# MLP up and FFN gate/value products as seven block products of summed weights

## The chip, the cores and the metric

One core of a Trainium2 chip runs the program. The time is the device time of one execution in microseconds (us), the median of the executions measured.

## The reference

Two transformer blocks over 512 tokens of width 1024, in float32. What matters here are three products with two factors each: the MLP of the first block and the gated FFN of the second block, which comes twice.

```python
m = rms_norm(h, mlp_norm[i])
h = h + jnp.square(jax.nn.relu(m @ w_mlp_up[i])) @ w_mlp_down[i]      # 1024 -> 4096 -> 1024
...
def conv_ffn(h, w_gate, w_val, conv_w, conv_b, w_out):               # 1024 -> 2816 -> 1024
    a = h @ w_gate
    ap = jnp.pad(a, ((0, 0), (CONV_W - 1, 0), (0, 0)))
    a = ap[:, 0:S] * conv_w[0] + ap[:, 1:S + 1] * conv_w[1] + ap[:, 2:S + 2] * conv_w[2] + conv_b
    return (jax.nn.silu(a) * (h @ w_val)) @ w_out
```

Everything else (gated linear attention, latent attention, pooling, chunked attention) stays as it is.

## The kernel before

The stages follow one another: mix, mlp, ple, pool, ffn0, att, ffn1. The residual x lies as 8 tiles of 128 features x 512 tokens (`x_...`). Products are made at float32 accuracy: each factor is split into a high part (rounded to fp32r) and a low part (what is left), and `mm3` (L328) sums high·high, high·low and low·high in one PSUM bank:

```python
mm(out, a[0], b[0], start=start, stop=False, skip_group_check=True)
mm(out, a[0], b[1], start=False, stop=False, skip_group_check=True)
mm(out, a[1], b[0], start=False, stop=stop, skip_group_check=True)
```

Weights come in units of 1024 columns (512 KB). `load_units` (L247) loads one into a tile `ws` from SyncE's queue, at most NL = 3 ahead. `split_unit` (L257) makes the parts in two halves: ACT copies `wh`, VectorE (DVE) subtracts `wl` (or GpSimd, POOL, where the planner finds that sooner: `sub`, L304). NW = 4 pairs exist, and after the first stage a unit is split at most two units before its use (`LAZY`).

At a stage's start `prep` (L376) takes each new x tile as it becomes final: `xsh` by ACT, `xsl` by DVE, squares, and POOL sums them (`sq`); from the sum comes the row R = 1/rms, which is multiplied in when a product is taken from PSUM. An up tile (128 outputs x 512 tokens, tile `pup`; `pf` for gate and value) is one unit: 8 k-blocks x 3 = 24 matmuls of 512 columns. `products` (L1162) runs a stage's first two tiles together, one k-block at a time; `mlp` (L1184) and `ffn` (L1348) take the others in groups of about eight tiles. From a gate tile come `fa`, the convolution `fb` (one ACT and two DVE instructions), its silu; from a value tile `fv`, the product with `fb`, and the split `yh`, `yl`. `down` (L1142) multiplies a group's results into 8 outputs (tile `pdn`), one unit each, after the next group's up tiles (`weave`, L1136), and `add_to` (L421) adds each output to its x tile. The last group's outputs start the next stage.

What each engine does, and in which order, is written by tasks (`spawn`, L185; `drive`, L197): Python generators with priorities that advance by the planner's own costs (`Pace`, L60). The engines then run these lists in order, so an instruction that waits holds all behind it on its engine. Nearly every instruction is recorded at the planner's line, L133 before and L144 after the change.

Of the kernel before, what the change touches and what calls it, by code (L numbers as in the profile page):

```python
# [16 lines left out]
P = 128  # L17
T = 512
# [27 lines left out]
G1 = groups(FF1 // P, 8)  # L46
G2 = groups(FF2 // P, 8)
# [12 lines left out]
class Pace:  # L60
# [21 lines left out]
    def note(self, engine, op, args, kw):  # L82
# [11 lines left out]
        elif engine == "vector":  # L94
            fast = op in ("tensor_copy", "tensor_scalar") and all(x.space == "SB" or "SB" in str(x.space) for x in aps)
            cost = 0.068 + (m if op == "tensor_reduce" else n) / (1920 if fast else 960)
            if any(n > 1 and x.free_size() == 1 for x in ins):
                cost += 0.063
        elif engine == "scalar":
            cost = 0.09 + n / 1190 + (0.093 if len(outs) > 1 or hasattr(kw.get("scale"), "tensor") else 0)  # L100
        elif engine == "gpsimd":
            cost = 0.23 + 0.165 * n if kw.get("op") == OP.pow else 0.1 + n / (350 if ins else 1400)
        else:
            cost = outs[0].shape[0] * n * 4 / 360e3
# [7 lines left out]
        if engine == "tensor":  # L112
            self.mine.add(outs[0].tensor.name)
        self.free[engine] = start + cost
# [5 lines left out]
        for x in outs:  # L120
            self.ready[x.tensor.name] = start + cost + (2.0 if engine == "sync" else 0.08)
# [22 lines left out]
class Norm:  # L144


    def __init__(self, gain):
        self.gain, self.xs, self.acc, self.count = gain, [None] * KD, None, 0
        self.ms = self.r = self.R = None

# [9 lines left out]

class Block:
    NS, N3, NSM = 64, 8, 48
    NW, NL = 4, 3
# [6 lines left out]
    HELP, TURN = 0.0, 1.0  # L170

    def __init__(self, ctx, tc, a):
# [9 lines left out]
        self.done, self.lazy = set(), self.LAZY[0]  # L182
# [42 lines left out]
    def slot3(self, name, dt=F32, shape=(P, 768)):  # L225
# [20 lines left out]

    def load_units(self, most=None):  # L247
        while self.n_load < min(self.n_split + self.NL, len(self.units)) and (most is None or self.n_load < most):
            src, cols = self.units[self.n_load]
            t = self.sp.tile([P, 1024], F32, tag="ws", bufs=self.NL, name="ws")  # L250
            if self.n_load >= self.NL:
                self.pace.ready[t.tensor.name] = self.split_at[self.n_load - self.NL]
            self.nc.sync.dma_start(t[:, :cols], src)
            self.loaded[self.n_load] = t
            self.n_load += 1

    def split_unit(self):  # L257
# [3 lines left out]
        cols = self.units[n][1]  # L261
        t = self.loaded.pop(n)
# [9 lines left out]
        self.split_at.append(self.pace.ready[l.tensor.name])  # L272
# [3 lines left out]
    def splitter(self):  # L276
        while self.n_split < len(self.units):
            yield lambda: self.n_split - self.n_free < self.NW and self.n_split - self.n_use < self.lazy
            self.load_units()
            yield [self.loaded[self.n_split]] + ([self.freed_by[self.n_split - self.NW]] if self.n_split >= self.NW else [])  # L280
            self.split_unit()

    def unit(self, *shape):
# [4 lines left out]
        cols = self.units[n][1]  # L288
# [15 lines left out]
    def sub(self, out, a, b):  # L304

        e = self.first((out, a, b), vector=(0.07, 1 / 960, 0), gpsimd=(0.1, 1 / 430, self.HELP))
        getattr(self.nc, e).tensor_sub(out, a, b)

    def mul(self, out, a, b):

        e = self.first((out, a, b), vector=(0.07, 1 / 960, 0), gpsimd=(0.1, 1 / 430, self.HELP))
# [64 lines left out]
    def prep(self, norm, d, x, row=True):  # L376
        yield [x]
        norm.xs[d] = self.hilo("xs", x, scale=self.col(norm.gain, d))
        self.square(norm, x, row)

# [747 lines left out]

    def units_mlp(self):
        a = self.a  # L1130
        ups = [[(a["w_up"][i], 1024) for i in g] for g in G1]
        downs = [[(a[f"w_down{gi}"][m], len(g) * 128) for m in range(KD)] for gi, g in enumerate(G1)]
        return self.weave(ups, downs)

    @staticmethod
    def weave(ups, downs):  # L1136
        out = list(ups[0])
        for i in range(1, len(ups)):
            out += ups[i] + downs[i - 1]
        return out + downs[-1]  # L1140

    def down(self, acts, after):  # L1142
        for m in range(KD):
            yield from self.unit(len(acts), 128)
            unit = self.got
            yield self.room()
            ps = self.bank("pdn")
            yield from self.fm(ps, unit, acts)
            self.used(ps)
            self.spawn(self.add_to(m, ps, after), 0)  # L1150
# [10 lines left out]

    def products(self, norm, name, finish, first):  # L1162

        if first:
            units = []
            for f in finish[:2]:
                yield from self.unit(8, 128)
                units.append(self.got)
            yield self.room()
            ps = [self.bank(name) for u in units]  # L1170
            for k in range(KD):
                yield norm.has(k)
                x = norm.xs[k]
                for i, u in enumerate(units):
                    yield [*u, *x]
                    self.mm3(ps[i], (u[0][:, k], u[1][:, k]), x, k == 0, k == KD - 1)
            for p, f in zip(ps, finish):
                self.used(p)
                self.spawn(f(p), 0)
            finish = finish[2:]  # L1180
        for f in finish:
            yield from self.product(norm, name, f)

    def mlp(self, norm, after):  # L1184
        v, s = self.nc.vector, self.nc.scalar

        def finish(acts, i, ps):
            yield norm.has_row
            yield [ps, norm.R]
            t = self.slot3("ht")[:, :T]  # L1190
            v.scalar_tensor_tensor(t, ps, 0.0, norm.R, op0=OP.max, op1=OP.mult)
            self.free()
            yield [t]
            s.activation(t, t, AF.Square)
            acts[i] = self.hilo("h", t)

        pend = None
        for gi, g in enumerate(G1):
            acts = [None] * len(g)
            yield from self.products(norm, "pup", [lambda ps, acts=acts, i=i: finish(acts, i, ps) for i in range(len(g))],  # L1200
                                     gi == 0)
            if gi == len(G1) - 1:
                norm.xs = None
                self.spawn(self.load_p(), 5)
            if pend is not None:
                yield from self.down(pend, lambda m: None)
            pend = acts
        yield from self.down(pend, after)
# [133 lines left out]
    def units_ffn(self, L):  # L1342
        a = self.a
        ups = [sum(([(a[f"w_fg{L}"][i], 1024), (a[f"w_fv{L}"][i], 1024)] for i in g), []) for g in G2]
        downs = [[(a[f"w_fo{L}_{gi}"][m], len(g) * 128) for m in range(KD)] for gi, g in enumerate(G2)]
        return self.weave(ups, downs)

    def ffn(self, L, norm, after):  # L1348
        v, s = self.nc.vector, self.nc.scalar
        cw = [lambda i, t=t: self.col(f"cw{L}", t * 22 + i) for t in range(3)]  # L1350

        def gate(i, ps, got):
            yield norm.has_row
            yield [ps, norm.R]
            a, b = self.slot3("fa")[:, :T], self.slot3("fb")[:, :T]
            v.tensor_mul(a, ps, norm.R)
            self.free()
            yield [a]
            s.activation(b, a, AF.Identity, scale=cw[2](i), bias=self.col(f"cb{L}", i))
            yield [b]  # L1360
            v.scalar_tensor_tensor(b[:, 1:], a[:, :T - 1], cw[1](i), b[:, 1:], op0=OP.mult, op1=OP.add)
            v.scalar_tensor_tensor(b[:, 2:], a[:, :T - 2], cw[0](i), b[:, 2:], op0=OP.mult, op1=OP.add)
            yield [b]
            s.activation(b, b, AF.Silu)
# [344 lines left out]
```

## Time and profile before

| | before |
|---|---|
| runs, median of three (lowest, highest) | 1692.51 us (1686.52, 1693.08) |
| the profiled execution: its own time | 1687.25 us |
| its span | 1685.5 us |
| TensorE (PE) busy, matmuls | 1654.5 us (98%), 8696 |
| DVE busy, instructions | 1006.8 us (60%), 1889 |
| ACT busy, instructions | 728.5 us (43%), 1422 |
| POOL busy, instructions | 192.0 us (11%), 206 |
| loads on SyncE's queue (q1) | 152.30 MB, 28.5% of 16 DMA engines |
| mean granted clock of PE | 0.998 |

Spans are of one execution; the time is that execution's own and lies 1.75 us above its span. A PE that is busy nearly all the time says that the other engines' busy shares are free until they make PE wait.

### The profile page before, as it was taken

The page shows a single profiled execution, that of the slowest core. Times are in us where ns is not written, and L with a number is a line of the kernel's source. Part 1 is how long each engine was busy: PE and PEld are TensorE (multiplying, and loading weights), DVE is VectorE, ACT ScalarE, POOL GpSimd, SP SyncE. Part 2 cuts the span into 40 slices and gives each one's busy share as a digit, 9 for nine tenths or more (in the row PEclk, how much of TensorE's full clock was granted, in tenths as well). Part 3 has the DMA queues.
Part 4 walks back from the last instruction along what each step waited for, and adds up shares of the span by engine and source line. Part 5 has one row for each costly group of instructions (what it writes and reads, how often), then busy time and mean ns, then how long its engine had stood idle before and what let it go on. Part 6 is the DMA issues. An engine that isn't in the chain of part 4 may idle for free. (4 is left out here: it accounts for less than half of the span.)

```text
span 1685.5 us, 22515 instructions
## 1 busy us (share of the span) xinstructions
PE 1654.5 (98%) x8696; PEld 1391.6 (83%) x8696; DVE 1006.8 (60%) x1889; ACT 728.5 (43%) x1422; POOL 192.0 (11%) x206
## 2 busy tenths in 40 slices
PE   8999999999999999999999999999999999999999
PEld 6878777888888888888888888999998788888887
DVE  6986777443434456776654645376678776644642
ACT  6746445432324245643332333375656543322321
POOL 3441302000000012200000001122221200000000
PEclk9999999999999999999999999999999999999999
DMA  6102032332333223233332332322131232333232
GB/s 214 63 26 63 16 123 75 100 101 87 102 99 113 88 88 104 75 100 98 91 111 88 96 98 94 113 76 89 64 99 53 81 101 94 100 106 95 93 98 72
DMA packets 47501, 153.73 MB, mean 91 GB/s; under 512 B 5521, under 2 KB 7458, under 8 KB 47394
## 3 DMA queue, kind: packets, MB, share of 16 engines
q1 hardware_dynamic: 47394, 152.30, 28.5%
q8 instruction: 68, 1.11, 0.3%
q14 instruction: 39, 0.32, 0.1%
HBM read 150.18 MB, written 2.10 MB: 90 GB/s over the span
## 5 line engine op out<-in xcount | busy, mean ns | idle before, releaser
L133 ACT ACTIVATE wh<-ws 128x512 fp32r<-128x512 f32 (+1 forms) x536 | 302.6, 613 | 254.7 <-PE pdn L133 214.0
L133 DVE TENSOR_TENSOR wl<-ws,wh 128x512 fp32r<-128x512 f32 (+1 forms) x508 | 341.6, 713 | 113.0 <-ACT wh L133 112.7
L133 PE MATMUL pf<-xsl,wh 128*128 128x512 f32 x704 | 275.1, 391 | 2.0 <-DVE xsl L133 2.0
L133 PE MATMUL pf<-xsh,wh 128*128 128x512 f32 x704 | 275.9, 392 | 0.0
L133 PE MATMUL pf<-xsh,wl 128*128 128x512 f32 x704 | 274.6, 390 | 0.0
L133 DVE TENSOR_TENSOR x<-x,pdn 128x512 f32<-128x512 f32 (+1 forms) x81 | 55.1, 681 | 219.1 <-PE pdn L133 219.1
L133 PEld LDWEIGHTS pf<-xsl,wh 128*128 128x128 f32 x704 | 132.6, 188 | 32.0 <-DVE xsl L133 4.3
L133 PEld LDWEIGHTS pf<-xsh,wh 128*128 128x128 f32 x704 | 132.5, 188 | 28.5 <-issue 0.5
L133 PEld LDWEIGHTS pf<-xsh,wl 128*128 128x128 f32 x704 | 132.5, 188 | 27.3
L133 PE MATMUL pdn<-yh,wh 128*128 128x512 f32 x352 | 136.9, 389 | 0.0
L133 PE MATMUL pdn<-yl,wh 128*128 128x512 f32 x352 | 136.9, 389 | 0.0
L133 PE MATMUL pdn<-yh,wl 128*128 128x512 f32 x352 | 136.9, 389 | 0.0
L133 POOL TENSOR_TENSOR sq<-sq 128x512 f32<-128x512 f32 x37 | 52.8, 1427 | 731.0 <-ACT sq L133 730.0
L133 PE MATMUL paq<-wh,xsh 128*128 128x256 f32 x384 | 111.3, 290 | 1.9 <-DVE akk L133 1.2
L133 PE MATMUL paq<-wl,xsh 128*128 128x256 f32 x384 | 108.5, 283 | 0.0
L133 PE MATMUL paq<-wh,xsl 128*128 128x256 f32 x384 | 108.5, 283 | 0.0
L133 PE MATMUL pup<-xsl,wh 128*128 128x512 f32 x256 | 99.7, 389 | 0.4 <-DVE xsl L133 0.4
L133 PE MATMUL pup<-xsh,wh 128*128 128x512 f32 x256 | 100.1, 391 | 0.0
L133 PE MATMUL pup<-xsh,wl 128*128 128x512 f32 x256 | 99.6, 389 | 0.0
L133 PE MATMUL pdn<-hh,wh 128*128 128x512 f32 x256 | 99.6, 389 | 0.0
L133 PE MATMUL pdn<-hl,wh 128*128 128x512 f32 x256 | 99.6, 389 | 0.0
L133 PE MATMUL pdn<-hh,wl 128*128 128x512 f32 x256 | 99.6, 389 | 0.0
(293 smaller groups left out, 3103.5 us busy)
## 6 DMA issues: line engine op xcount, KB each, us to landing
ws<-in_w_fg SPq DMA_DIRECT2D x44, 512.0 KB, 3.6
ws<-in_w_fv SPq DMA_DIRECT2D x44, 512.0 KB, 3.6
ws<-in_w_up SPq DMA_DIRECT2D x32, 512.0 KB, 3.5
ws<-in_w_down SPq DMA_DIRECT2D x32, 512.0 KB, 3.5
ws<-in_w_fo SPq DMA_DIRECT2D x32, 448.0 KB, 3.3
ws<-in_w_fo SPq DMA_DIRECT2D x16, 512.0 KB, 3.5
ws<-in_w_out SPq DMA_DIRECT2D x8, 512.0 KB, 3.6
ws<-in_w_gate SPq DMA_DIRECT2D x8, 512.0 KB, 3.6
```

The lines of the kernel that those rows point to most:

```text
L133: return call(*args, **kw)
```

## The change

Four up tiles make a quad. With x as 2 x 2 blocks (k-blocks 0-3 and 4-7, tokens 0-255 and 256-511) and the weights of a quad as 2 x 2 blocks (k-blocks 0-3 and 4-7, output tiles 0-1 and 2-3), the 2 x 2 block product is made from seven products of sums instead of eight. Each is a phase: one unit of weights (a block, or a sum of blocks) times 4 k-blocks of 256 columns: 4 x 2 x 3 = 24 matmuls of 256 columns. Where a phase stands on an older result, that one is first taken from PSUM by an ACT copy (`c1`, `u2`, `u4`), and DVE combines.

- The first four tiles of each stage are done plainly and together (`first_tiles`): 96 matmuls of 512 columns, one k-block of four banks at a time. The other 28 tiles of mlp are 7 quads, the other 40 of each FFN 10 quads: 27 quads in all.
- Sums of weight blocks are made by DMA: a tile is loaded plainly, and other blocks are added into it by accumulating DMAs, which POOL issues. Per quad: 5 plain loads and 4 accumulating ones (one into `low`; into `sum` one at its load, one after the split of phase 2, one after that of phase 3) in place of 4 plain loads.
- `prep_blocks` builds the sums and differences of x blocks at a stage's start and splits them.
- The results of four tiles (mlp: one quad; FFN: two quads, since half of a quad's tiles are gates) are one down group. A down unit gives two outputs of four terms, and is woven in after phases 4, 3, 2 and 6 of the quads of the next group, as far as there are units: after phases 3 and 4 in most FFN quads, after all four in the mlp and in the ninth quad of an FFN, after phase 4 alone in quads 0, 1 and 9. x tiles are added to 64 times in mlp (32 before) and 56 times in each FFN (24 before).
- NL becomes 7, the 512-wide slots 55 (64 before), and after the first stage POOL no longer takes subtractions or products (`HELP`).

```diff
-    NS, N3, NSM = 64, 8, 48
-    NW, NL = 4, 3
+    NS, N3, NSM = 55, 8, 48
+    NW, NL = 4, 7
...
-    HELP, TURN = 0.0, 1.0
+    HELP, TURN = (0.0, 1e3), 1.0
...
+QG1 = [1] * (FF1 // P // 4)
+QG2 = [1] + [2] * (FF2 // P // 4 - 1) + [1] * 2
+
+PHASES = (("b11", 0, True, "a11"), ("b21", 1, True, "a12"), ("n3", 2, True, "sum"), ("n2", 0, False, "sum"),
+          ("n1", 0, False, "low"), ("b22", 0, False, "sum"), ("t4", 2, False, "a22"))
+
+LOADS = (("sum", 0, -2, (2,)), ("a11", 0, 0, ()), ("a12", 1, 1, ()), ("low", 2, 2, (3,)), ("a22", 3, 5, ()))
+
+ADDED = {2: 3, 3: 1}
...
+    def load_units(self, most=None):
...
+                n.tile[name] = t
+                for block in more:
+                    self.nc.gpsimd.dma_start(t, n.src[block], accum_op=OP.add)
...
+    def split_unit(self):
...
+            if ph in ADDED:
+                nc.gpsimd.dma_start(t, quad.src[ADDED[ph]], accum_op=OP.add)
...
+    def blocks_high(self, norm, k, x, col, h, l):
...
+        n, c = self.slot("xn"), self.slot("xc")
+        self.scaled(n, x, col)
+        nc.vector.scalar_tensor_tensor(c[:, L], low[:, R], -1.0, n[:, R], op0=OP.mult, op1=OP.subtract)
+        nc.vector.tensor_add(c[:, R], c[:, L], low[:, L])
+        nc.vector.tensor_add(n[:, L], n[:, L], c[:, L])
...
+    def quads(self, norm, order, sizes, last, after, take, finish):
...
+            if first:
+                yield self.room()
+                ps[acc] = self.bank("pq%d" % acc)
+            else:
+                name = (None, None, None, "c1", "u2", "u4", "c22")[i]
+                yield lambda: name in quad
+                yield [quad[name]]
+            b = norm.blocks[block]
+            for k in range(4):
+                yield lambda: b[k] is not None
+                for w in range(2):
+                    yield [*unit, *b[k]]
+                    self.mm3(ps[acc][:, w * 256:(w + 1) * 256], (unit[0][:, 4 * w + k], unit[1][:, 4 * w + k]), b[k],
+                             first and k == 0 and w == 0, k == 3)
...
+    def quad_step(self, i, ps, quad):
...
+        if i in (0, 3, 4):
+            name = {0: "c1", 3: "u2", 4: "u4"}[i]
+            t = self.slot(name)
+            s.activation(t, ps[0], AF.Copy)
+            quad[name] = t
+        if i == 1:
...
+            v.tensor_add(t, ps[1], t)
...
+        elif i == 4:
+            yield [t, ps[2]]
+            v.tensor_sub(t, ps[2], t)
+            quad["c22"] = t
...
+        elif i == 6:
+            t = quad["u2"]
+            yield [t, ps[2]]
+            v.tensor_sub(t, ps[2], t)
```

**In the middle of ffn1, on DVE.** Names: `qr` is a pair of result tiles (`qr_16430` the two value tiles of a quad, `fb_...` their gates), `pq0` to `pq2` the three banks, `ws_16121` the tile of `sum`. Before, one gate and one value tile:

```order
L133 TENSOR_TENSOR fa_12976<-pf_12924,R_12456 128x512
L133 SCALAR_TENSOR_TENSOR fb_12977<-fa_12976,cols_63,fb_12977 128x511
L133 SCALAR_TENSOR_TENSOR fb_12977<-fa_12976,cols_63,fb_12977 128x510
L133 TENSOR_TENSOR wl_13006<-ws_12891,wh_13005 128x512 x2
L133 TENSOR_TENSOR fv_13016<-pf_12964,R_12456 128x512
L133 TENSOR_TENSOR fv_13016<-fv_13016,fb_12977 128x512
L133 TENSOR_TENSOR yl_13023<-fv_13016,yh_13022 128x512
```

Now, from the last half of a quad's value tiles to their low parts, in the next quad:

```order
L144 TENSOR_TENSOR qr_16430<-u2_16351,R_14583 128x2x256
L144 TENSOR_TENSOR wl_16579<-ws_16121,wh_16578 128x512 x2
L144 TENSOR_TENSOR qr_16430<-qr_16430,fb_16501 128x512
L144 TENSOR_TENSOR wl_16597<-ws_16342,wh_16596 128x512 x2
L144 TENSOR_TENSOR c1_16563<-pq1_16558,c1_16563 128x512
L144 TENSOR_TENSOR yl_16624<-qr_16430,yh_16623 128x512
L144 TENSOR_TENSOR qr_16430<-qr_16430,fb_16536 128x512
L144 TENSOR_TENSOR wl_16635<-ws_16306,wh_16634 128x512 x2
L144 TENSOR_TENSOR qr_16643<-c1_16563,R_14583 128x2x256
L144 TENSOR_TENSOR wl_16671<-ws_16416,wh_16670 128x512 x2
L144 TENSOR_TENSOR yl_16679<-qr_16430,yh_16678 128x512
```

The split `wl_16579` of the sum for phase 3, made from what an accumulating DMA has added to, now stands ahead of the 13 instructions that end with the last low part of the values.

**At the start of ffn1.** DVE before, from the row's mean square to the first gates:

```order
L133 TENSOR_SCALAR ms_12415<-pst_12410 128x4
L133 TENSOR_TENSOR wl_12430<-ws_12270,wh_12429 128x512 x2
L133 TENSOR_SCALAR dg_12437<-ident_65,r_12417 128x128 x4
L133 TENSOR_TENSOR fa_12464<-pf_12331,R_12456 128x512
L133 TENSOR_TENSOR fv_12467<-pf_12332,R_12456 128x512
```

DVE now, the same stretch (`xc`, `xt`: sums of x blocks):

```order
L144 TENSOR_SCALAR ms_14506<-pst_14501 128x4
L144 TENSOR_TENSOR xcl_14511<-xc_14428,xch_14510 128x512
L144 TENSOR_TENSOR xt_14514<-xn_14427,xt_14514 128x256
L144 TENSOR_TENSOR wl_14527<-ws_14097,wh_14526 128x512 x2
L144 TENSOR_SCALAR dg_14549<-ident_65,r_14508 128x128 x4
L144 TENSOR_TENSOR wl_14567<-ws_13781,wh_14566 128x512 x2
L144 TENSOR_TENSOR xsl_14247<-xn_14252,xsh_14246 128x256
L144 TENSOR_TENSOR xsl_14259<-xn_14266,xsh_14258 128x256
L144 TENSOR_TENSOR xsl_14293<-xn_14300,xsh_14292 128x256
L144 TENSOR_TENSOR xsl_14319<-xn_14326,xsh_14318 128x256
L144 TENSOR_TENSOR qr_14560<-pf_14332,R_14583 128x512
```

Work on x blocks stands between the row and the first results, and more of it ahead of this stretch. From the first `xsl` to the low part that the first down output waits for, DVE's list holds 88 instructions in ffn1 and 86 in ffn0. POOL's list there is now

```order
L144 TENSOR_TENSOR sq_14250<-sq_14250,sq_14371 128x512
L144 DMA ws_14414<-in_w_f1 128x1024
L144 TENSOR_TENSOR r_14508<-ms_14506,mhalf_72 128x4
L144 DMA ws_13781<-in_w_f1 128x1024 x2
L144 DMA ws_14655<-in_w_f1 128x1024
```

where an accumulating DMA stands before the power that gives R, and four to a quad follow.

**At the end of ffn1, on DVE.** Before, splits and additions took turns, and all activations were long made:

```order
L133 TENSOR_TENSOR wl_14777<-ws_14688,wh_14776 128x448 x2
L133 TENSOR_TENSOR x_2706<-x_2706,pdn_14745 128x512
L133 TENSOR_TENSOR wl_14807<-ws_14720,wh_14806 128x448 x2
L133 TENSOR_TENSOR x_2769<-x_2769,pdn_14775 128x512
L133 TENSOR_TENSOR x_2797<-x_2797,pdn_14805 128x512
```

Now, from the last quad's seventh phase on:

```order
L144 TENSOR_TENSOR u2_17747<-pq2_17677,u2_17747 128x512
L144 SCALAR_TENSOR_TENSOR fb_17892<-qr_17706,cols_63,fb_17892 128x511
L144 SCALAR_TENSOR_TENSOR fb_17892<-qr_17706,cols_63,fb_17892 128x510
L144 TENSOR_TENSOR x_2789<-x_2789,pdn_17881 128x512
L144 TENSOR_TENSOR qr_17794<-u2_17747,R_14583 128x2x256
L144 TENSOR_TENSOR x_2815<-x_2815,pdn_17898 128x512
L144 TENSOR_TENSOR x_2878<-x_2878,pdn_17908 128x512
L144 TENSOR_TENSOR qr_17794<-qr_17794,fb_17862 128x512
L144 TENSOR_TENSOR x_2986<-x_2986,pdn_17917 128x512
L144 TENSOR_TENSOR yl_17930<-qr_17794,yh_17929 128x512
L144 TENSOR_TENSOR qr_17794<-qr_17794,fb_17892 128x512
L144 TENSOR_TENSOR yl_17938<-qr_17794,yh_17937 128x512
```

Between the last phase and the last down units only one down unit (four outputs) is left for PE.

## Rows read from the trace of the kernel before

**Rows 1.** The page, part 1: busy time, share of the span, instructions of each engine

```profile
PE 1654.5 (98%) x8696; PEld 1391.6 (83%) x8696; DVE 1006.8 (60%) x1889; ACT 728.5 (43%) x1422; POOL 192.0 (11%) x206
```

**Rows 2.** Waits of PE: for what, us in total, times, longest

```profile
PE pl L133 <- ACT wh L133: 8.4, 1, 8.4
PE pf L133 <- DVE xsl L133: 2.0, 3, 0.8
```

**Rows 3.** Stretches, PE alone: length, busy us (matmuls), granted clock, DMA share, GB/s

```profile
264.00:282.00 18.00, 15.87 (x71) 1.00 0.19 58
694.00:706.00 12.00, 10.77 (x48) 1.00 0.28 89
1314.00:1336.00 22.00, 20.05 (x83) 0.92 0.27 84
1325.00:1330.00 5.00, 3.05 (x17) 1.00 0.48 156
1330.00:1335.00 5.00, 5.00 (x17) 0.66 0.32 104
```

**Rows 4.** The chain that ended last: start, us, engine, tile, instructions

```profile
1336.24 149.64 PE pf L133 x660
1605.56 76.17 PE pdn L133 x336
```

**Rows 5.** PE's timeline in att, 256 columns each: start, us, operation

```profile
1064.00 0.28 PE L133 MATMUL paq<-wh,xsl 128*128 128x256 f32 x1
1067.96 0.28 PE L133 MATMUL paq<-wh,xsl 128*128 128x256 f32 x1
```

**Rows 6.** The page: loads (KB, us from issue to landing); SyncE's queue (packets, MB, share)

```profile
ws<-in_w_fg SPq DMA_DIRECT2D x44, 512.0 KB, 3.6
q1 hardware_dynamic: 47394, 152.30, 28.5%
```

**Rows 7.** DVE's timeline in the middle of ffn1: start, us, operation, count [idle before]

```profile
1405.90 1.54 DVE L133 SCALAR_TENSOR_TENSOR fb<-fa,cols,fb 128x511 f32<-128x511 f32 x2 [0.88 <-ACT fb L133]
1408.71 1.29 DVE L133 TENSOR_TENSOR wl<-ws,wh 128x512 fp32r<-128x512 f32 x2 [1.28 <-ACT wh L133]
1410.64 0.69 DVE L133 TENSOR_TENSOR fv<-fv,fb 128x512 f32<-128x512 f32 x1
```

**Rows 8.** ACT's timeline, the same stretch

```profile
1405.05 0.81 ACT L133 ACTIVATE fb<-fa,cols 128x512 f32<-128x512 f32 x1 [2.88 <-DVE fa L133]
1411.37 0.63 ACT L133 ACTIVATE yh<-fv 128x512 fp32r<-128x512 f32 x1 [2.17 <-DVE fv L133]
```

**Rows 9.** Groups by form: ACT copy of a bank; DVE on 256 columns (mean ns)

```profile
L133 ACT ACTIVATE aqkv<-paq 128x512 f32<-128x512 f32 x8 | 4.8, 602 | 0.0
L133 DVE TENSOR_TENSOR ogl<-pot,ogh 128x256 fp32r<-128x256 f32 x8 | 3.0, 418 | 2.3 <-PE pw L133 2.0 <-ACT ogh L133 0.2
```

**Rows 10.** DVE's timeline: the first low part of x in mlp, ffn0, ffn1

```profile
257.78 0.75 DVE L133 SCALAR_TENSOR_TENSOR xsl<-x,cols,xsh 128x512 fp32r<-128x512 f32 x1 [0.79 <-ACT xsh L133]
691.19 0.75 DVE L133 SCALAR_TENSOR_TENSOR xsl<-x,cols,xsh 128x512 fp32r<-128x512 f32 x1 [0.84 <-ACT xsh L133]
1308.86 0.75 DVE L133 SCALAR_TENSOR_TENSOR xsl<-x,cols,xsh 128x512 fp32r<-128x512 f32 x1 [0.85 <-ACT xsh L133]
```

**Rows 11.** PE's timeline: the first matmul of mlp, ffn0, ffn1

```profile
265.35 0.39 PE L133 MATMUL pup<-xsh,wh 128*128 128x512 f32 x1
694.84 0.48 PE L133 MATMUL pf<-xsh,wh 128*128 128x512 f32 x1
1316.50 0.39 PE L133 MATMUL pf<-xsh,wh 128*128 128x512 f32 x1
```

**Rows 12.** DVE's timeline at ffn1's start, beside POOL's `sq` additions and after them

```profile
1311.71 3.48 DVE L133 SCALAR_TENSOR_TENSOR xsl<-x,cols,xsh 128x512 fp32r<-128x512 f32 x2
1319.88 2.89 DVE L133 TENSOR_TENSOR wl<-ws,wh 128x512 fp32r<-128x512 f32 x2
1323.35 1.28 DVE L133 TENSOR_TENSOR wl<-ws,wh 128x512 fp32r<-128x512 f32 x2
```

More of the change, by code (lines that the diff above doesn't have):

```diff
@@ L149, in __init__ @@
         self.ms = self.r = self.R = None
+        self.low, self.blocks = [None] * 4, {p[0]: [None] * 4 for p in PHASES}
+        self.plain = False
     def has(self, k):
@@ new lines, in first_tiles @@
+    def first_tiles(self, norm, take, acts):
+        yield self.room(3)
+        ps = [self.bank("pf") for w in range(4)]
+        for u in range(4):
+            yield from self.unit(8, P)
+            unit = self.got
+            for k in range(2 * u, 2 * u + 2):
+                yield lambda: norm.xs[k] is not None
+                for w in range(4):
+                    yield [*unit, *norm.xs[k]]
+                    i = 4 * (k % 2) + w
+                    self.mm3(ps[w], (unit[0][:, i], unit[1][:, i]), norm.xs[k], k == 0, k == KD - 1)
+            self.used(ps[3])
+        norm.plain = ps[3]
+        self.spawn(self.first_out(norm, ps, take, acts), 0)
@@ new lines, in quad_row @@
+    def quad_row(self, quad, r, half, src):
+        norm = quad["norm"]
+        yield norm.has_row
+        yield [src, norm.R]
+        if quad["rows"][r] is None:
+            quad["rows"][r] = self.slot3("qr")
+        cs = slice(half * T // 2, (half + 1) * T // 2)
+        out = quad["rows"][r].rearrange("p (w n) -> p w n", w=2)[:, :, cs]
+        quad["take"](out, src.rearrange("p (w n) -> p w n", w=2), norm.R[:, None, cs].to_broadcast([P, 2, T // 2]))
+        quad["left"][r] -= 1
+        if quad["left"][r] == 0:
+            self.spawn(self.finish(quad["acts"], quad["rows"], r, quad["at"]), 0)
@@ L1129, in units_mlp, with down @@
+    def down(self, acts, u, after):
+        n = len(acts)
+        yield from self.unit(8, P)
+        unit = self.got
+        for i in range(8 // n):
+            yield self.room()
+            ps = self.bank("pdn")
+            yield from self.fm(ps, unit, acts, i * n, n)
+            if i == 8 // n - 1:
+                self.used(ps)
+            self.spawn(self.add_to(8 // n * u + i, ps, after), 0)
     def units_mlp(self):
         a = self.a
-        ups = [[(a["w_up"][i], 1024) for i in g] for g in G1]
@@ L1132, in units_mlp @@
[L1132 to L1150, printed above, removed]
+        at, downs = 0, []
@@ L1160, in product @@
         self.spawn(finish(ps), 0)
[L1162 to L1208, printed above, removed]
     def units_ple(self):
@@ L1393, in units_att @@
+        gates = {}
+        yield from self.quads(norm, self.order["ffn", L], QG2, 2, after, self.mul, finish)
+        norm.blocks = None
     def units_att(self):
@@ L1510, in attention @@
         self.att = self.va = self.qk = None
+    QUADS = ("mlp", "ffn0", "ffn1")
     STAGES = ("mix", "mlp", "ple", "pool", "ffn0", "att", "ffn1")
```

307 lines of the change are left out of this document (238 added, 69 removed).

## The prediction

> **What bounds the kernel now.** I read the busy shares first. PE is busy 98% of the span, DVE 60%, ACT 43%, POOL 11% [rows 1]. The waits of PE come next: the longest is 8.4 us at the program's start, and the FFN tiles wait for DVE three times, 2.0 us together [rows 2]. So only two things can move the time: PE's own work, and waits that the change makes. The stretches show what PE loses at the starts of mlp, ffn0 and ffn1 [rows 3]: 18.00 - 15.87 = 2.1, 1.2, and 22.00 - 20.05 = 1.95. After ffn1's gap the granted clock is 0.66 over the next 5 us, part of them at 1.2 GHz instead of 2.4: 5 x 0.34 = 1.7 us more. Together the three starts lose 7.0.
>
> **What PE saves.** The chain gives 660 gate/value matmuls of 512 columns in 149.64 us and 336 down matmuls in 76.17: 0.2267 us each [rows 4]. For 256 columns there is the qkv product in att: 33 starts between 1064.00 and 1067.96, 0.120 us each [rows 5]. A quad replaces 96 x 0.2267 = 21.76 us by 168 x 0.120 = 20.16. It saves 1.6, not the eighth that the count of products suggests, because 256 columns cost more than half of 512. 27 quads: **-43.3 us**. The down work and the four first tiles keep their matmuls.
>
> The Trainium skill ("TensorE: Matmul & The Clock Gate", Back-to-back issue gap) gives N/2.4 + 2.5 ns for an isolated matmul of N columns: 109 and 216 ns, so 64 us saved. The rows, at 120 and 227 ns, speak against it, and its own text says that the formula under-counts at small N.
>
> **The unknown: an accumulating DMA.** None is in the trace. L is the time from its issue to its landing. A plain 512 KB load lands after 3.6 us [rows 6]. All of the queue's 152.30 MB take 28.5% of 16 engines over 1685.5 us, so 0.524 MB take 1.65 us of all 16. Below, L cannot be under 3.6, since the transfer does all that a load does and also reads its target. Above I take three full passes: 3.6 + 2 x 1.65 = 6.9. One more read alone gives 5.25. In an FFN quad, 7 plain loads (two are down units) and 4 accumulating ones of two passes take 7 x 1.65 + 4 x 3.3 = 24.8 us out of 7 x 2.88 + 2 x 5.44 = 31.0 us of PE's time: 80%, where 28.5% was. So every second transfer finds a plain load ahead of it, +0.8. I take **L = 6.0**.
>
> The Trainium skill ("Collectives: The Full Stack", The bandwidth ceiling) says that an add in the DMA path needs two source reads and runs at half the rate of a copy. By it alone L would be 5.25 and the sum below about 12 us lower.
>
> **What L costs in the FFNs.** Let t = 0 be where PE begins phase 0 of a quad (a phase is 24 x 0.120 = 2.88). Prices on DVE: 0.60 for one of 512 columns in a row (1.29 for two, 0.69 alone), 1.54 for a pair of convolution steps [rows 7]; on ACT 0.81 and 0.63 [rows 8]. The bank of the quad before is complete at -2.88; take, ACT, convolution pair and the split of `sum` for phase 2 follow one another and end at 1.7. Then POOL issues the next addition into `sum`, which lands at 1.7 + L. ACT splits a half (0.66 with handover), and DVE works through the list shown, from `wl_16579` to `yl_16679`: 14 instructions, 13 x 0.60 + 0.69 = 8.5. The last low part exists at L + 10.9.
> - In the first quad of a two-quad group PE wants it after four phases and 10 matmuls of the down output, 11.5 + 2.3 = 13.8. Stall L - 2.9 = 3.1; three quads in each FFN: **+18.6**.
> - Phase 3 itself needs the second half of that split at 1.7 + L + 0.66 + 1.29 and asks for it at 3 x 2.88 + 0.6 = 9.24: stall L - 5.6 = 0.4 in 12 other FFN quads: **+4.8**.
> - The two ninth quads carry four down units. I take half of 3.1 each: **+3.2**.
>
> In mlp a down unit stands between phases 2 and 3 and covers both.
>
> **Small waits.** Phase 4 needs the ACT copy of phase 3's bank. Where no down unit lies between, PE waits for handover, 0.60 [rows 9] and handover, 0.85. Five such places outside the starts: **+4.3**.
>
> **Stage ends.** After the last quad's phase 6 one down unit is left, 24 x 0.2267 = 5.44, and the next needs the last activations. From phase 5's bank on, DVE's list (the third place shown) runs without a break, with two ACT steps in between, and ends 10.1 us after phase 6 in ffn1, 11.3 in ffn0 (one more split). PE gets there at 5.44 + 0.9. Stalls of 3.8 and 5.0: **+8.8**. Before there was no such wait, since eight tiles' outputs covered it.
>
> **Stage starts.** DVE's list from the first `xsl` to the low part that the first down output needs holds 88 instructions in ffn1, 86 in ffn0, 69 in mlp. At 0.60 each, 0.67 for `xsl`, and 0.33 for 256 columns (0.418 alone [rows 9], less the 0.09 that overlaps), this is 44.7, 44.0 and 33.6 us. Beside POOL's additions DVE is stretched: two `xsl` 3.48, a split pair 2.89, against 1.28 after them [rows 12]; I add 5 us per start. Counted from the first `xsl` [rows 10] the parts are there at 1358.6, 740.2 and 296.4 on the clock of before. PE starts [rows 11] at 1316.50, 694.84, 265.35, does 96 x 0.2267 = 21.8 of first tiles, then five phases and 0.9 in an FFN (37.1), three phases and 2.3 in mlp (32.7): 1353.6, 731.9, 298.1. Lost 5.0, 8.3 and 0, that is 13.3 in place of 7.0: **+6.3**.
>
> **Clock.** ffn1's start shows that a gap of 1.95 us can be followed by 1.7 us of loss at 1.2 GHz [rows 3]; mlp's of 2.1 was not. Ten of the stalls above are longer. I count the four long ones and half of the six: 7 x 1.7 = **+12**.
>
> **At nothing.** DVE's 96 added additions lie beside PE: in a middle FFN quad its list is 37 instructions, 22.4 us of PE's 31. POOL's subtractions that move to DVE are a dozen after the first stage, 7 us if nothing covered them. Plain loads run ahead with NL = 7.
>
> **Sum.** -43.3 + 18.6 + 4.8 + 3.2 + 4.3 + 8.8 + 6.3 + 12 = +14.7. The profiled execution took 1687.25, so 1702.0. The median of the runs is 1692.51, 5.3 above it; I forecast **1704**. With L at 6.9 the sum is 24.0 + 15.6 + 4.0 + 4.3 + 8.8 + 6.3 + 17 - 43.3 = +36.7, 1724 to 1729. With 5.25 it is near +3. The forecast's own range is 1690 to 1730.
>
> **Rivals.**
> - *The additions land like loads, and the lists keep up.* At L = 3.6 the first group quads stall 0.7 each (4.2), the others not at all; ninth quads 0.8, small waits 4.3. With ends and starts as reckoned and four slow spells (6.8) that is -12, 1675 to 1680. If DVE's lists also end in time at starts and ends, -41: 1646 to 1651. For it: loads are fast and queues were 28% used. Against: an addition does more, and 24.8 of 31 us would be busy. It decides where L falls below 4.5. Chance 0.27.
> - *DMA becomes the bound.* At three passes a quad wants 7 x 1.65 + 4 x 4.95 = 31.4 us of all engines, more than PE's 31.0. Then transfers queue, L = 9: 6 x 6.1 + 12 x 3.4 + 2 x 3.0 + 19.4 + 22 spells x 1.7 - 43.3 = +97, about 1787. Chance 0.09.
> - *256 columns run at 109 ns.* Saving 64 instead of 43.3: sum -6, 1681 to 1686. The rows speak against it: 0.03.
> - *The phases run slower than in att.* The 33 starts of the price are one burst. At 0.130 us 27 x 168 x 0.01 = 45 us eat the whole saving: +60, about 1750. Chance 0.04.
>
> **How the numbers follow.** A measurement of this kernel can tell about 0.5%, 8.4 us, from no change. The forecast's case holds 0.57: slower 0.36, same 0.18, faster 0.03. The first rival gives faster 0.25 and same 0.02, the next slower 0.09, then same 0.01 and faster 0.02, the last slower 0.03 and same 0.01. Faster 0.30, same 0.22, slower 0.48. The range 1664 to 1740 takes in the bounds of L and the near half of the first rival.
>
> **What would show it.** Right: quads at 0.120 us a matmul; PE waits named `yh`, `yl` before `pdn` in quads 2, 4, 6 of each FFN, near 3 us; accumulating DMAs landing 5 to 7 us after issue; about 4 us at each FFN's end; granted clock dips behind these. Wrong: L under 4.5, or PE's waits under 30 us in all, or over 90.

## The result and the profile after

The changed kernel takes 1763.47 us (median of 4 runs, 1756.83 to 1766.94) against 1692.78 for the kernel before in the same session: ratio 1.0422, interval 1.0382 to 1.0462. It is slower, as forecast, but by 71 us instead of 12, and outside the range.

The page after, its line on the engines, the two DMA queues (packets, MB, share of 16 engines) and two kinds of loads (KB, us to landing); they answer to [rows 1, 6]:

```profile
PE 1656.2 (94%) x10640; PEld 1475.1 (84%) x10640; DVE 1235.1 (70%) x2321; ACT 879.1 (50%) x1708; POOL 267.6 (15%) x306
q1 hardware_dynamic: 50706, 166.46, 27.2%
q0 software_dynamic: 15552, 56.63, 18.9%
ws<-in_w_f SPq DMA_DIRECT2D x108, 512.0 KB, 4.3
ws<-in_w_f POOLq DMA_DIRECT2D x80, 512.0 KB, 5.5
```

By the forecast PE was to lose 43 us of work, yet it is as busy as before (1656.2 us) in a longer span: idle time has grown from 31 to 104 us, and part of the work ran at the lower clock. An accumulating DMA (POOL's queue, q0) lands 5.5 us after its issue; a plain load in the FFNs now takes 4.3 instead of 3.6. The mean granted clock is 0.979 over 1760.5 us, where it was 0.998 over 1685.5: 1760.5 x 0.021 - 1685.5 x 0.002 = 37.0 - 3.4 = 33.6 us of full-speed time more that PE was not given. At the lower level, half of the higher, it spent twice that, some 67 us more. The 33.6 are the most that this can have cost, since a part of it lies in idle time.

By stage, PE alone (stretch, its length, busy us with the matmuls recorded, granted clock, DMA share, GB/s). Before: mix, mlp, ffn0, att, ffn1:

```profile
0.00:265.40 265.40, 248.83 (x1521) 0.99 0.25 84
265.40:630.70 365.30, 363.17 (x1605) 1.00 0.31 96
694.80:1058.60 363.80, 362.57 (x1598) 1.00 0.31 97
1058.60:1316.50 257.90, 252.90 (x2026) 1.00 0.25 80
1316.50:1685.50 369.00, 363.27 (x1595) 0.99 0.29 93
```

After, the same five:

```profile
0.00:271.70 271.70, 248.84 (x1520) 0.99 0.28 92
271.70:638.70 367.00, 356.45 (x2109) 0.99 0.51 144
702.20:1099.70 397.50, 368.15 (x2317) 0.96 0.59 152
1099.70:1363.50 263.80, 255.42 (x2025) 1.00 0.25 81
1363.50:1760.50 397.00, 363.81 (x2315) 0.97 0.57 146
```

mlp is 1.7 us longer. The FFNs are 33.7 and 28.0 longer, with 29 and 33 us in which PE does nothing, and a granted clock of 0.96 and 0.97. The first stage and the attention stage, which have no new products, are 6.3 and 5.9 longer.

What PE waits for after (us in total, times, longest):

```profile
PE pq L144 <- ACT u L144: 29.9, 7, 4.7
PE pdn L144 <- DVE yl L144: 12.7, 13, 2.4
PE pdn L144 <- ACT yh L144: 12.1, 11, 3.0
```

**The wait that was not foreseen.** Seven times PE stands 3.4 to 4.7 us before phase 4 for the copy `u2` of phase 3's bank. The prediction gave this copy 0.85. ACT's timeline in the second quad of ffn1 (phase 3 ends on PE at 1437.1):

```profile
1432.32 1.15 ACT L144 ACTIVATE wh<-ws 128x512 fp32r<-128x512 f32 x2 [5.25 <-DMA ws<-in_w_f]
1434.38 2.18 ACT L144 ACTIVATE wh<-ws 128x512 fp32r<-128x512 f32 x4
1437.56 0.63 ACT L144 ACTIVATE yh<-qr 128x512 fp32r<-128x512 f32 x1 [1.00 <-DVE qr L144]
1440.11 1.15 ACT L144 ACTIVATE wh<-ws 128x512 fp32r<-128x512 f32 x2 [1.92 <-DMA ws<-in_w_f]
1441.17 0.58 ACT L144 ACTIVATE u<-pq 128x512 f32<-128x512 f32 x1
```

and PE's next matmul, the first of phase 4:

```profile
1441.80 0.58 PE L144 MATMUL pq<-xsh,wh 128*128 128x256 f32 x1 [4.66 <-ACT u L144]
```

At 1437.6 ACT makes one `yh` and could then copy the bank, 0.58 us of work. But its next instruction is `wh`, the split of the sum for phase 5, and that waits for an accumulating DMA until 1440.1. The copy stands behind it. The bank was complete all that time, and PE has lost 4.66 us. In five of the seven places ACT waits like this, for 1.5 to 4.1 us. In the quads 0 of the two FFNs it waits for the addition only 0.4 and 0.5 us; there the copy is late mainly because ACT's own list ahead of it is long (PE waits 3.7 and 3.4).

**What the clock adds.** The same place in stretches of 4 us:

```profile
1434.00:1438.00 4.00, 3.14 (x25) 1.00 0.49 72
1438.00:1442.00 4.00, 0.20 (x1) 0.80 0.95 306
1442.00:1446.00 4.00, 4.00 (x19) 0.50 0.81 175
1446.00:1450.00 4.00, 4.00 (x20) 0.84 0.86 238
```

After the gap PE is busy without a break and does so at 0.50, the 1.2 GHz level, before it is given 2.4 GHz again. In this profile each of the seven gaps has such a slow spell at its end or behind it (0.66 to 0.83 over the ten us around them).

**The wait that was foreseen.** DVE in the fifth quad of ffn1, from the last half of the values to their last low part:

```profile
1527.86 0.69 DVE L144 TENSOR_TENSOR qr<-u,R 128x512 f32<-128x512 f32 x1
1532.21 1.29 DVE L144 TENSOR_TENSOR wl<-ws,wh 128x512 fp32r<-128x512 f32 x2 [3.66 <-ACT wh L144]
1533.42 0.69 DVE L144 TENSOR_TENSOR qr<-qr,fb 128x512 f32<-128x512 f32 x1
1540.04 0.68 DVE L144 TENSOR_TENSOR yl<-qr,yh 128x512 fp32r<-128x512 f32 x1
```

The split for phase 3 comes 3.66 us after the instruction ahead of it, and the activations follow behind. The chain shows its cause and its end, and, last, 144 matmuls of six phases in a row:

```profile
1526.20 5.33 DMA ws<-in_w_f
1540.12 0.61 DVE yl L144
1540.78 3.47 PE pdn L144 x14
1552.59 17.43 PE pq L144 x144
```

The addition is issued at 1526.20 and lands 5.33 later; at 1540.78 PE resumes, after 2.4 us. By the prediction's formula, L - 2.9, this is 2.43. Six phases take 17.43 us, 0.121 a matmul, close to the price of 0.120. Four of the six stalls of this kind, 2.4 us each, have no slow spell behind them; one of the four, in ffn0, with the ten us around it:

```profile
942.00:952.00 10.00, 7.61 (x42) 1.00 0.82 233
```

### The profile page after: what moved, and what is told of

The parts are those of the page before. It is cut to its first block, busy times and chain, and to the rows that moved or that the text cites. A ratio compares the mean times of both kernels' runs of the same rounds, so it can differ in the third digit from the quotient of the medians.

```text
span 1760.5 us, 27639 instructions
## 1 busy us (share of the span) xinstructions
PE 1656.2 (94%) x10640; PEld 1475.1 (84%) x10640; DVE 1235.1 (70%) x2321; ACT 879.1 (50%) x1708; POOL 267.6 (15%) x306
## 3 DMA queue, kind: packets, MB, share of 16 engines
q1 hardware_dynamic: 50706, 166.46, 27.2%
q0 software_dynamic: 15552, 56.63, 18.9%
## 5 line engine op out<-in xcount | busy, mean ns | idle before, releaser
L144 ACT ACTIVATE wh<-ws 128x512 fp32r<-128x512 f32 x690 | 390.3, 620 | 342.6 <-PE pdn L144 131.3
L144 DVE TENSOR_TENSOR wl<-ws,wh 128x512 fp32r<-128x512 f32 x683 | 450.9, 702 | 153.1 <-ACT wh L144 152.5
L144 PE MATMUL pq<-xsh,wh 128*128 128x256 f32 x864 | 251.8, 291 | 29.9 <-ACT u L144 29.9
L144 PE MATMUL pq<-xsh,wl 128*128 128x256 f32 x864 | 250.5, 290 | 0.0
L144 PE MATMUL pq<-xsl,wh 128*128 128x256 f32 x864 | 250.4, 290 | 0.0
L144 PEld LDWEIGHTS pq<-xsh,wh 128*128 128x128 f32 x864 | 171.8, 199 | 34.1 <-ACT u L144 31.3
L144 PEld LDWEIGHTS pq<-xsl,wh 128*128 128x128 f32 x864 | 171.8, 199 | 2.7 <-issue 0.5
L144 POOL DMA_DIRECT2D ws<-in_w_f x80 | 70.5, 884 | 667.6 <-DVE wl L144 350.6
L144 PEld LDWEIGHTS pq<-xsh,wl 128*128 128x128 f32 x864 | 171.8, 199 | 0.0
L144 PE MATMUL pdn<-yl,wh 128*128 128x512 f32 x352 | 143.7, 408 | 12.7 <-DVE yl L144 12.7
L144 PE MATMUL pdn<-yh,wh 128*128 128x512 f32 x352 | 143.0, 406 | 12.1 <-ACT yh L144 12.1
L144 PE MATMUL pq<-xch,wh 128*128 128x256 f32 x432 | 122.9, 285 | 3.8 <-ACT wh L144 2.3
L144 PE MATMUL pq<-xch,wl 128*128 128x256 f32 x432 | 123.9, 287 | 0.8 <-DVE wl L144 0.7
```

The lines of the kernel that those rows point to most:

```text
L144: return call(*args, **kw)
```

## The experiments

Ratios are to the kernel before, in the same session; a difference between two kernels in us is that of their ratios, times 1692.

**1. The copy ahead of the split.**

```diff
...
+            u = self.units[n]
+            if isinstance(u[0], str) and u[2] == 5:
+                yield lambda: "u2" in u[1].made
             yield [self.source(n)] + ([self.freed_by[n - self.NW]] if n >= self.NW else [])
...
+            if i == 3:
+                quad["load"].made[name] = True
...
```

> The changed kernel with one rule more: the split of the sum for phase 5 is recorded only after the copy u2 of the same quad, so on ACT the copy stands ahead of the split instead of behind it. In the changed kernel PE waits 29.9 us in seven places for u2, 4.3 us each. Theory (the lists): the copy is held by the split ahead of it, which waits for an accumulating DMA. Then these waits fall to 0.85 each, 6 us, the granted clock has about seven slow spells of 3.4 us fewer (1.7 us each), and the time falls by 24 + 12 = 36 us, 30 to 45. Rival (the additions themselves): phase 5 is late with its sum anyway, so PE waits the same 30 us one phase later, named wh or wl, and the time stays within 8 us.

Measured: 1737.68 us, ratio 1.0283 (1.0257 to 1.0309), 24 us less than the change's 1.0422. PE's waits:

```profile
PE pdn L144 <- DVE yl L144: 12.0, 10, 2.4
PE pq L144 <- ACT u L144: 9.1, 7, 2.2
```

The 29.9 us have become 9.1, and nothing of that size took their place: PE's idle time in the profile falls by 21.5 us in all. In the two traces the lists of DVE, POOL and SyncE are the same, and ACT's differs in these seven places alone: so it is the list, and not the additions as such. But the mean clock of the profile is 0.981, hardly better than 0.979 (0.981 to 0.984 over the four runs, against 0.973 to 0.979), so of the 12 us expected from slow spells little came.

**2. A later landing in the planner.**

```diff
-            self.ready[x.tensor.name] = start + cost + (2.0 if engine == "sync" else 4.0 if op == "dma_start" else 0.08)
+            self.ready[x.tensor.name] = start + cost + (2.0 if engine == "sync" else 6.5 if op == "dma_start" else 0.08)
```

> The changed kernel with the planner's estimate of an accumulating DMA's landing raised from 4.0 to 6.5 us after POOL's part. Nothing is added or taken away; on DVE the activations (product, high and low part) of the first quad of a group now stand ahead of the split of the sum for phase 3, and in the quads 0 the copy u2 stands ahead of the split for phase 5. Theory (the lists): the six stalls before a group's first down output, 2.4 to 2.8 us each, 15 in all, go, and two of the seven u2 waits (8 us) fall to 0.85 each; with some eight slow clock spells of 1.7 us fewer the time falls by 15 + 6 + 13 = 34, 20 to 40 us. Rival (the additions themselves): phase 3 gets its split later by what the activations take, and PE waits there instead; the time stays within 8 us.

Measured: 1738.67 us, ratio 1.0297 (1.0276 to 1.0318), 21 us less.

```profile
PE pq L144 <- ACT u L144: 24.1, 7, 4.7
PE pdn L144 <- ACT yh L144: 9.8, 8, 3.0
PE pdn L144 <- DVE yl L144: 1.0, 4, 0.3
```

The waits for `yl` fall from 12.7 to 1.0 and those for `yh` from 12.1 to 9.8, by the order of the lists alone. ACT's list changes too, and in the two quads 0 the copy `u2` comes in time, as expected (29.9 to 24.1). The clock does not recover (0.978); the profile of the change shows why for four of the stalls, which had no slow spell behind them.

**3. No additions at all.**

```diff
-                for block in more:
-                    self.nc.gpsimd.dma_start(t, n.src[block], accum_op=OP.add)
...
-            if ph in ADDED:
-                nc.gpsimd.dma_start(t, quad.src[ADDED[ph]], accum_op=OP.add)
```

> The changed kernel without any accumulating DMA: the weight sums are left out, each sum tile holds its first block alone. Everything else, order of the lists included, is the same. Theory (all large waits hang on the additions' landing): the u2 waits fall to 0.85 each, the stalls at group starts to nothing, with their slow spells: 24 + 15 + 25 = 64 us less, about 1700; what is left over the kernel before is stage starts, stage ends and the attention stages. Rival (the engines' lists are too long, whatever lands when): DVE and ACT still end late and the time falls by less than 25 us.

Measured: 1698.96 us, ratio 1.0061 (1.0041 to 1.0081), 61 us less. ffn0 and ffn1:

```profile
697.60:1066.00 368.40, 355.72 (x2317) 0.98 0.34 110
1330.10:1698.70 368.60, 355.38 (x2315) 0.98 0.32 103
```

As the theory had it: 61 of the 71 us go when nothing has to land. (The sums are left out, so the products are not the reference's; the time alone is of use.) The run is less clean than was expected, though. Without the additions the planner also puts other instructions at about 160 places of DVE's list and 100 of ACT's, so the 61 us are not the landing alone. At the place shown above ACT's order is still the changed kernel's, the copy behind the split, and there the split does not wait:

```profile
1397.61 0.63 ACT L144 ACTIVATE yh<-qr 128x512 fp32r<-128x512 f32 x1 [0.93 <-DVE qr L144]
1398.40 1.15 ACT L144 ACTIVATE wh<-ws 128x512 fp32r<-128x512 f32 x2 [0.16 <-PE pq L144]
1401.39 0.60 ACT L144 ACTIVATE u<-pq 128x512 f32<-128x512 f32 x1 [1.84 <-PE pq L144]
```

The rest is as instructive. With no addition to wait for, the FFNs are only as long as before (368.4 against 363.8, 368.6 against 369.0): each loses some 13 us of idle time at its start, its end and in `u2` copies that nothing covers, and some more to the clock, about what the products save.

**4. The settings alone.** The kernel before with

```diff
-    NS, N3, NSM = 64, 8, 48
-    NW, NL = 4, 3
+    NS, N3, NSM = 58, 8, 48
+    NW, NL = 4, 6
...
-    HELP, TURN = 0.0, 1.0
+    HELP, TURN = (0.0, 1e3), 1.0
...
```

> The kernel before with the new settings alone, as far as they go into memory with its products: 58 slots of 512 instead of 64 (the change has 55), loads up to 6 ahead instead of 3 (the change 7), POOL without subtractions and products after the first stage. In the changed kernel the first stage is 6.4 us longer and the attention stage 5.8, though no product there is touched. Theory: the settings do it, through other orders in the lists, so this kernel is 6 to 14 us slower than the kernel before, in those two stages. Rival: it comes from the neighbouring new stages (first loads and x blocks), and this kernel is within 3 us of the one before.

Measured: 1698.16 us, ratio 1.0050 (1.0032 to 1.0069). The first stage takes 271.0 us and the attention stage 262.6, against 265.4 and 257.9 before.

The theory holds: about 9 us (5 to 12) are the price of the settings, as far as this kernel has them, in the two stages without new products.

**5. Both list edits.** The diffs of 1 and 2 together.

> The two list edits together on the changed kernel (the copy u2 ahead of the split for phase 5; the later landing in the planner, which puts the activations ahead of the split for phase 3). Each alone took about 23 us off. Theory (two separate places, each with its own waits and slow spells): the gains add up, less the two u2 places in the quads 0 that both mend, 40 us off the changed kernel, 1.7% over the kernel before, 1.4 to 2.0%. Rival (one shared limit behind both, the additions): the second edit gives less than 8 us on top of the first, 2.4 to 2.8% over the kernel before.

Measured: 1708.12 us, ratio 1.0100 (1.0085 to 1.0115): 54 us off the changed kernel. That is 10 us more than the two alone (24 + 21), though by the four intervals together this surplus is known only to some 9 us. The same place as above on ACT, then ffn0 and ffn1, and the engines:

```profile
1408.47 0.63 ACT L144 ACTIVATE yh<-qr 128x512 fp32r<-128x512 f32 x1 [1.00 <-DVE qr L144]
1409.01 0.58 ACT L144 ACTIVATE u<-pq 128x512 f32<-128x512 f32 x1
1410.62 1.16 ACT L144 ACTIVATE wh<-ws 128x512 fp32r<-128x512 f32 x2 [1.03 <-DMA ws<-in_w_f]
```

```profile
700.40:1073.50 373.10, 358.71 (x2318) 0.98 0.62 162
1337.10:1704.50 367.40, 352.46 (x2315) 0.99 0.61 158
```

```profile
PE 1636.6 (96%) x10640; PEld 1461.0 (86%) x10640; DVE 1237.3 (73%) x2321; ACT 878.6 (52%) x1708; POOL 266.2 (16%) x306
```

The copy now follows `yh` at once, and the split waits behind it. ffn1 is 1.6 us shorter than before the change, ffn0 9.3 longer. From run 2 to this one, five copies move ahead of their splits on ACT, and no other list changes. The `u2` waits fall by 17.5 us (24.1 to 6.6) and the time by 33 (29 to 38 by the intervals). The rest is the clock: the same 10640 matmuls keep PE busy for 1636.6 us instead of 1651.8, at a mean clock of 0.988 instead of 0.978. Run 1's edit, on lists that still had the stalls on DVE, had shortened the busy time by only 2.4. All additions are still there: 54 of the 71 us were lost to the order of the lists and the clock behind it.

**6. The down unit after phase 3.**

```diff
-                        for _ in range((4, 3, 2, 6)[:min(most, len(wait))].count(ph)):
+                        for _ in range((3, 4, 2, 6)[:min(most, len(wait))].count(ph)):
```

> Both list edits, and the order in which down units are woven in begins with phase 3 instead of phase 4, so in quads 0, 1 and 9 of an FFN and the last quad of mlp the one down unit covers the copy u2. Theory: what is left of the u2 waits (about 0.8 in each of seven places, 6 us) and some slow spells behind them go; 6 to 15 us below the kernel with both list edits. Rival: the down unit asks for activations 2.9 us earlier in those quads, and in quad 0 these are the last of the stage's start; then PE waits there instead and the time is the same within 4 us or worse.

Measured: 1717.77 us, ratio 1.0167 (1.0141 to 1.0194), 11 us worse than 5. The rival holds: the down unit asks for activations that are not there (run 5: 10.9 us, longest 3.0). Nor do the `u2` waits go; they are 8.9 us in 13 places, after 6.6 in seven.

```profile
PE pdn L144 <- ACT yh L144: 16.0, 5, 5.6
```

**7. Splits three ahead.**

```diff
-    LAZY = 3, 2
+    LAZY = 3, 3
```

> Both list edits, and units are split up to three before their use after the first stage too, instead of two (four pairs exist). The additions into the sums can then start a phase earlier, 2.9 us. Theory (the additions' landing still binds in what is left): PE's waits for the splits and the activations behind them shrink, 5 to 15 us below the kernel with both list edits. Rival (the landing no longer binds, stage starts and ends do): within 4 us, or worse by up to 10 where earlier splits push activations back on ACT and DVE.

Measured: 1766.10 us, ratio 1.0435 (1.0414 to 1.0457), 57 us worse than 5 and far outside both expectations. Two of PE's waits, and ACT at ffn0's start:

```profile
PE pdn L144 <- ACT yh L144: 32.0, 13, 6.7
PE psr L144 <- DVE dg L144: 12.4, 3, 9.1
```

```profile
739.17 1.15 ACT L144 ACTIVATE wh<-ws 128x512 fp32r<-128x512 f32 x2 [9.22 <-DMA ws<-in_w_f]
```

A split that may be recorded earlier is recorded earlier, and then ACT stands 9.22 us before it until its addition has landed, with the copies of the x blocks and the row R behind it. It is the fault of the changed kernel, made larger.

**8. Kept warm.** 30 matmuls that nobody reads behind phase 3, in the seven places of the `u2` wait:

```diff
...
+            if i == 3 and units_after(order, step):
+                self.keep_busy(30, unit, b)
...
```

> The changed kernel with 30 extra matmuls of 256 columns (3.6 us) behind phase 3 in the seven places where PE waits 4.3 us for u2; they go into a spare bank and nobody reads them. All other lists are the same. Theory (the granted clock falls behind such gaps, and that costs on top of them): PE's idle time falls by 25 us with no gain of itself, seven or more slow spells of 3.4 us go, and the time falls by 12 us, 8 to 20. Rival (the clock falls for other reasons, or slow spells only lie where PE would wait anyway): within 4 us of the changed kernel.

Measured: 1750.30 us, ratio 1.0347 (1.0330 to 1.0365), 13 us less. ffn0 and ffn1, 180 extra matmuls among them:

```profile
702.20:1090.30 388.10, 371.69 (x2408) 0.97 0.60 156
1354.90:1749.00 394.10, 373.48 (x2405) 0.97 0.57 147
```

More work and a shorter time, with the lists of ACT, DVE, POOL and SyncE the same as in the changed kernel: the clock behind the gaps is a cost of its own. PE's busy time rises by 17 us where 210 x 0.120 = 25 were added. Not all of it comes back: the four stalls of 2.4 us for `yl`, which had cost no clock in the changed kernel, now have slow spells. The one shown above:

```profile
938.00:948.00 10.00, 7.62 (x30) 0.83 0.82 221
```

**9. POOL's share given back, an input loaded earlier** (on 5).

```diff
+            if step == len(order) - 12 and sizes is QG1:
+                self.spawn(self.load_p(), 5)
...
-        self.spawn(self.load_p(), 5)
...
-            self.lazy, self.help = self.LAZY[1], self.HELP[1]
+            self.lazy = self.LAZY[1]
+            self.help = self.HELP[i + 1 < len(stages) and stages[i + 1] in self.QUADS]
```

> Both list edits, POOL allowed to take subtractions and products again in the stages without quads (attention, PLE, pooling), and the per-layer input loaded and split before the last quad of mlp is done instead of after all of it. In the kernel with both list edits the attention stage is 5.7 us longer than before the change and PE waits 3.2 and 0.6 us for that input. Theory (the setting and the late load are what is left there): the attention stage falls to 258 to 260 us, the two waits go with a slow spell, together 6 to 12 us less, within 0.3 to 0.7% of the kernel before. Rival (the longer attention stage comes from the order of its loads, not from POOL): only the waits go, 3 to 6 us.

Measured: 1715.50 us, ratio 1.0140 (1.0121 to 1.0159), worse than 5. The attention stage takes 263.0 us, about as long as in the changed kernel (263.8). The wait for the input is gone, but the copies `u2` make PE wait 13.7 us where run 5 had 6.6; why is open, since many places of the lists differ.

**10. Three loads ahead in the first stage** (on 9).

```diff
-        while (self.n_load < len(self.loads) and self.n_load - len(self.ws_freed) < self.NL
+        while (self.n_load < len(self.loads) and self.n_load - len(self.ws_freed) < self.most
```

`self.most` is 3 in the first stage and NL after it (those lines are left out here).

> As the last, and in the first stage loads run only three units ahead, as in the kernel before. Theory (the first stage is 4.6 to 6.4 us longer because of the seven): it falls by 4 to 6 us to about 265, and the whole is within 0.3% of the kernel before. Rival (the 55 slots or the new neighbours do it): the first stage stays at 269 to 272 us.

Measured: 1719.41 us, ratio 1.0176 (1.0150 to 1.0202). The first stage took 276.8 us, longer than either expectation: the theory falls.

**11. Fewer slots in the kernel before.** NS = 58 alone.

> The kernel before with 58 slots of 512 instead of 64 and nothing else (three loads ahead, POOL as before). Of the three settings, POOL's share and the loads ahead have been tried with the change and gave nothing back. Theory (the slots, which set the order of the lists and what waits for a slot to be given up): the first stage is about 271 us and the attention stage 262 to 263, as with all settings, the whole 6 to 12 us slower than the kernel before. Rival (the loads ahead): within 3 us of the kernel before, both stages at 265 and 258.

Measured: 1690.66 us, ratio 1.0004 (0.9992 to 1.0015). First stage and attention take 268.2 and 258.2 us in its profile.

In this kernel the slots are not it: with 58 of them every engine's list is the one of before, so 268.2 against 265.4 is scatter between executions. What the 55 slots do to the lists of the changed kernel was not tried. The attention stage is 258.2 with three loads ahead in it (here) and 262.6 to 263.8 with six or seven (4, 9, the change), with POOL's help or without. So the loads ahead remain as its cause, by exclusion; they were not tried alone. Which setting lengthens the first stage stays open.

**12. Kept warm in what is left** (on 5): 10 and 14 extra matmuls before two down units of each FFN, 24 at the end of mlp.

> The kernel with both list edits, and extra matmuls of 256 columns that nobody reads in five of its longest gaps that are left: 10 ahead of the first down output of each FFN, 14 ahead of the last group's first down output of each FFN, 24 at the end of mlp. Theory (slow spells follow these gaps): three to six spells of 1.7 us go, 5 to 10 us less than with the list edits alone, 0.4 to 0.7% over the kernel before. Rival (the spells that are left come from the starts' many small waits): within 4 us of the kernel with the list edits.

Measured: 1708.89 us, ratio 1.0126 (1.0103 to 1.0149): no gain over 5. The lists of the other engines are the same, and the mean clock rose from 0.988 to 0.994, which is worth some 10 us; 72 extra matmuls at 0.120 take 8.6. That they ate the gain, standing in the path themselves, is an inference.

No version that has the block products with their sums beats the kernel before; the best, 5, is 1.0% above it.

## Why the prediction was wrong

Step by step, with what the profile after and the runs showed:

- **What PE saves, -43.3.** Held nearly: 0.121 us a matmul, so 27 x (21.76 - 168 x 0.121) = 38.7. The rivals on the matmul's price (0.109, 0.130) are out.
- **L = 6.0.** Measured 5.5 in the FFNs and 5.4 in mlp. Per byte the additions hold the engines twice as long as plain loads: 18.9% for 56.63 MB is 0.334 a MB, against 27.2 / 166.46 = 0.163. This agrees with the half rate that the Trainium skill ("Collectives: The Full Stack", The bandwidth ceiling) gives for the add in a ring step; by it alone the prediction estimated L at 5.25, nearer than its 6.0. Neither bound nor the rival of saturated DMA engines was reached.
- **The stalls from L, +18.6, +4.8, +3.2.** Mechanism right, seen in the chain. The six stalls at group starts are 2.4 to 2.8 each, 15 in all, for 18.6. Phase 3 itself waited for its split in two FFN quads, 0.6 and 1.5 us, not in twelve; the ninth quads did not wait.
- **Small waits, +4.3: the step that failed first.** The prediction priced the copy `u2`, in five places, as if ACT were free when phase 3 ended. What stood ahead of it in ACT's list was not read; it was a split that waits for a second addition. The waits are 29.9 us instead, in seven places (7.1 of them in the two quads 0, where ACT's own work is most of it). Run 1 settles it.
- **Clock, +12: the step that failed next.** It was up to 33.6, nearly three times that. The prediction counted seven slow spells of 1.7 us each. The seven missed gaps each had one of their own, and after three of them it lost twice 1.7. The stalls that were counted by half, six at group starts, had two. The same four stalls without a spell have one in run 8: whether a gap of 2.4 us costs clock depends on what lies around it, in a way that stays open. Runs 5 and 8 show the clock as a cost of its own.
- **At nothing.** NL = 7 and POOL's share were given nothing. The settings cost 9 us in run 4, and the two stages without new products are 12 longer in the profile after; run 11 shows no part of the slots in it. An input that mlp loads at its end now, and no longer before its last down units, made PE wait 3.2 us more.
- **Ends +8.8 and starts +6.3.** Right in kind, too large in size: the ends took 3.0 and 2.3 us, and before its first down output PE waited 1.7 in each FFN where 5.0 and 8.3 were reckoned, after a `u2` wait in the same quad that was not. With no additions (run 3) the FFNs still lose some 13 us each of idle time.

So the direction was right and the stalls that the forecast named were there, but its +14.7 was a small difference of large terms, and most of the 71 us came from what it had mis-sized. The two failed steps and the settings, 25.6 + 21.6 + 12, are about the 59 us that were missing; the other terms missed by a few us each, in both directions, so this is a tally and not a proof. That run 5, at 1708, comes near the forecast's 1704 is luck: its lists also lack the stalls that the forecast had priced at 18.6. The lists as the forecast supposed them, with the copy in time and the split for phase 3 ahead of the activations, are nearest to run 1's, and that takes 1738.

## What to carry to other kernels

When an edit puts a slow arrival (here a second and third addition into one tile) into an in-order list, read the lists of every engine for what stands behind the instruction that waits for it, not only that of the engine that uses the result; here ACT's list cost as much as DVE's, and each was mended by an order alone. A planner that believes in an early landing puts the wait ahead of ready work, and here looking further ahead made it worse (run 7). And price gaps on PE together with the slow clock behind them: here mending one kind gave back little more than the waits, and mending the second as well gave back the clock too.

## What the hardware showed that was not expected

- After a gap of 4.66 us PE ran the next 4 us at a granted clock of 0.50 while it was busy throughout; seven times 3.6 us of matmuls that nobody reads made the kernel 13 us faster.
- The same stall of 2.4 us, in the same place of the same lists, was passed at a granted clock of 1.00 in the changed kernel and at 0.83 over ten us in run 8, where other gaps had been filled.
- An accumulating DMA of 512 KB costs POOL 0.88 us (70.5 for 80) and lands after 5.5. Plain loads in the FFNs land after 4.3 us beside these, and after 3.3 in run 3, which leaves them out.
- Two list edits that gave 24 and 21 us alone gave 54 together; the surplus of 10 is known to some 9 us.
